# Causal masks added on VectorE within the maximum, and the two smallest query tiles scored over both branches at once

## The chip, the cores and the metric

The kernel runs on one core of a Trainium2 chip. A core has five engines that work beside each other, each through its own queue of instructions in order: TensorE (PE; its weight loads are shown apart as PEld), VectorE (DVE), ScalarE (ACT), GpSimd (POOL) and SyncE (SP), which issues DMA transfers. TensorE writes its products into PSUM, a small memory of eight banks of 2 KB per partition; everything else lives in SBUF. The metric is the time of one execution on the device in microseconds, as the median of several runs.

## The reference

One layer of a hybrid decoder is computed for two groups of tokens: a prompt of 1024 tokens, and 8 sampled sequences of 8 tokens each that have 2048 earlier tokens in a paged cache. The layer is half a SwiGLU, then a mixer of attention heads and Mamba-2 heads side by side, then another half SwiGLU. The attention has three branches that share queries: compressed blocks, selected blocks and a sliding window. What the change touches is the masked softmax of the last two, for the prompt:

```python
def masked_softmax(s, mask):
    s = jnp.where(mask, s.astype(jnp.float32), NEG)
    e = jnp.where(mask, jnp.exp(s - jnp.max(s, axis=-1, keepdims=True)), 0.0)
    return e / jnp.maximum(jnp.sum(e, axis=-1, keepdims=True), 1e-30)
...
    s = s - slopes[None, :, :, None, None] * dist      # window branch
    mask = (dist >= 0) & (dist < WINDOW) & (k_pos >= 0)[None, :]
```

There are 8 query heads over 2 key/value heads, 64 wide. The prompt has 1024 tokens in selection blocks of 64, that is 16 blocks, and 16 are selected, so that for the prompt the selected branch is plain causal attention over all earlier keys; the window branch sees the last 512. For the sampled sequences the compressed branch also needs summaries of the cached rows: blocks of 32 rows at a stride of 16 go through a small two-layer network (`compress`).

## The kernel before

**The stage.** The change lies in the attention stage, about 1130 to 1550 us of the execution. Two bodies of work are interleaved in it. The first is the prompt's attention, in 8 query tiles of 128 tokens (the program's `qt`), taken in the order 2, 7, 6, 5, 4, 3, 1, 0 (`KN["qt"]`). The second is the compression of the cached rows of the 8 sampled sequences (`compress_sample`): `KN["cs"]` = 3, 0, 2, 1, 1, 0, 1, 0 says how many sequences are written into the program ahead of each tile.

**A query tile.** First the scores of the compressed branch for all heads, `s_cmp`, with their mask (L1770) and softmax. Then for each of the 2 key/value heads and each of the two other branches (`br` 0 all earlier keys, `br` 1 the window) come the 4 query heads. A head's keys are 128(qt+1) for branch 0 and at most 640 for branch 1, cut into one or two pieces of at most 512 columns, each piece in a PSUM bank `s2` of which there are three. A piece is written by a product of the leading parts (L1808, `KA`, `QA`), a product of the small parts with the ALiBi slopes (L1810, `KB`, `QB`), and, where it has a masked block, a product of an identity with a mask in bf16 (L1813): `mdiag` for the last 128 columns, where the keys meet the queries, `medge` for the first 128 of the window. Then VectorE takes the maximum (L1818 for one piece; L1821 per piece and L1822 to join two), ScalarE the exponential straight from PSUM into the tile `pb` (L1824) with the row sums, one engine chosen by a table scales `pb` by gate and sum (L275 to L279), TensorE transposes it (L1846, `pT`), and products with the values (L1855, `o`) close the head group.

**A sequence's compression.** A gather of 128 rows of the paged cache (L1689, `chk`, one buffer), then eight times: two copies (`chp`, L267), four transposes (`cT`, L1712), the transposes' high part `th` on ScalarE (L267) and low part `tl` on VectorE (L1717), and 12 products `cA` (L1733 to L1735). After four of these the hidden layer (`cxh`) and two products `c` (L1740 for keys, L1743 for values) follow.

**What sets the order.** The program is written for a framework that lists instructions in its own order, by priorities and estimates, before the run; each engine then works through its list in order. The waits between engines follow from the tiles.

**The next stage** is the sampled sequences' attention with the output projection (`wout`, L250 to L252). Its buffers lie in the space of the compression weights `w1h` and `w1l` and of the other tiles of this stage: the window keys `schk` (L2052), the constants `big` (L1951), the residual `xT` (L1892, added to `wout` at L1939) and the weights `raw` (L1900) are loaded there.

## Time and profile before

| what | value |
|---|---|
| median of 3 runs | 2470.73 us (2468.52 to 2479.9) |
| profiled execution | 2475.45 us, its span 2473.8 us |
| mean granted clock of TensorE | 0.987 |
| busy share | PE 97%, DVE 71%, ACT 46%, POOL 17% |
| attention stage, 1130 to 1490 us | PE busy 349.4 of 360 us, DVE 226.4, ACT 235.0, POOL 143.3 |
| mask products in the stage (L1813) | 160, mean 235 and 232 ns from start to modelled end |
| maxima in the stage (L1818, L1821) | 64 and 128 |

Two readings need care. The granted clock is the share of TensorE's full speed that the chip let it have: at 0.50 every product takes twice as long, and a busy TensorE then is not one at its best. And matmuls overlap each other, so that the mean of one, as the groups show it, is longer than the time by which it delays the next; that time is read from start to start in the rows of the timeline.

### The profile page before, as it was taken

To read this page: it belongs to the slowest core of one execution; us is meant where nothing else is said; L and a number is where in the kernel's file an instruction comes from. 1 tells how busy PE (TensorE), PEld (TensorE's weight loads), DVE (VectorE), ACT (ScalarE), POOL (GpSimd) and SP (SyncE) were. 2 spreads that over 40 slices of the span, in tenths; PEclk is the share of its full clock that TensorE was granted. 3 is DMA by queue.
4 is the path that set the end of the run, shared out by engine and by line. 5 is a ranking of instruction groups with operands and counts; after the bars stand their busy time and mean duration, and the time that the engine had idled before them with its cause. 6 is when DMAs were issued, how large, how long until landed. Compare 5 with 4: busy or idle time off the path is not lost.

```text
span 2473.8 us, 48193 instructions
## 1 busy us (share of the span) xinstructions
PE 2408.8 (97%) x19026; PEld 2222.8 (90%) x19026; DVE 1744.7 (71%) x3673; ACT 1131.2 (46%) x2501; POOL 418.3 (17%) x533
## 2 busy tenths in 40 slices
PE   7999999999999999999999999999999999999998
PEld 6999999999999998997667766677899999999998
DVE  6777776677778855655656666777967676768776
ACT  7544444441133254425666675444545454543113
POOL 0000000011134343333434343111000000001110
PEclk9999999999999999999999998999999999999999
DMA  4334343598652333423110104476235353559654
GB/s 162 134 133 160 130 164 129 175 338 306 230 190 84 126 116 102 119 69 127 40 64 35 69 35 148 130 250 213 89 123 171 120 174 120 174 213 370 238 209 153
DMA packets 230446, 379.07 MB, mean 153 GB/s; under 512 B 18509, under 2 KB 147705, under 8 KB 228812
## 3 DMA queue, kind: packets, MB, share of 16 engines
q1 hardware_dynamic: 210248, 318.02, 37.7%
q0 software_dynamic: 7600, 38.59, 4.5%
q10 hardware_dynamic: 12372, 19.38, 2.2%
q8 instruction: 150, 2.46, 0.4%
q14 instruction: 76, 0.62, 0.1%
HBM read 255.66 MB, written 124.40 MB: 154 GB/s over the span
## 4 chain that ended last, share of the span: by engine, by line
PE 86%; DVE 6%; DMA 4%; ACT 3%; issue 1%; POOL 0%; ACTq 0%; DVEq 0%; POOLq 0%
PE dq L634 6%; PE gY L367 6%; PE dq L633 6%; PE dq L635 6%; PE gY L368 6%; PE gY L366 6%; PE gX L367 5%; PE gX L366 5%; PE gX L368 5%; PE o L1855 3%; PE pT L1846 3%; PE s L1808 1%; PE xbc L250 1%; PE xbc L251 1%; PE xbc L252 1%; PE cA L1733 1%
## 5 line engine op out<-in xcount | busy, mean ns | idle before, releaser
L634 PE MATMUL dq<-db,da 128*128 128x256 f32 (+1 forms) x1232 | 353.2, 288 | 0.3 <-DVE da L270 0.3
L635 PE MATMUL dq<-db,da 128*128 128x256 f32 (+1 forms) x1232 | 352.8, 288 | 0.0
L633 PE MATMUL dq<-db,da 128*128 128x256 f32 (+1 forms) x1232 | 349.8, 288 | 2.7 <-DVE Cc L386 2.2
L642 DVE TENSOR_TENSOR xT<-xT,dq 128x256 f32<-128x256 f32 (+1 forms) x456 | 186.9, 432 | 84.8 <-PE dq L635 83.2
L270 POOL TENSOR_TENSOR ds<-dw 128x512 f32<-128x512 f32 x22 | 29.5, 1341 | 1228.1 <-DVE wlo L270 508.0
L633 PEld LDWEIGHTS dq<-db,da 128*128 128x128 f32 x1232 | 230.5, 189 | 3.3 <-DVE Cc L386 2.5
L635 PEld LDWEIGHTS dq<-db,da 128*128 128x128 f32 x1232 | 232.8, 189 | 0.0
L634 PEld LDWEIGHTS dq<-db,da 128*128 128x128 f32 x1232 | 231.9, 188 | 0.6 <-DVE da L270 0.5
L267 ACT CAST whi<-ws 128x512 fp32r<-128x512 f32 x156 | 96.5, 623 | 205.9 <-PE gY L368 137.6
L270 DVE TENSOR_TENSOR wlo<-raw,whi 128x512 fp32r<-128x512 f32 x184 | 125.5, 687 | 83.9 <-ACT whi L267 83.5
L267 ACT CAST da<-ds 128x512 fp32r<-128x512 f32 x88 | 52.6, 623 | 234.7 <-PE dq L635 93.4
L267 ACT CAST whi<-raw 128x512 fp32r<-128x512 f32 x181 | 112.4, 626 | 72.0 <-PE g L414 19.5
L270 DVE TENSOR_TENSOR wlo<-ws,whi 128x512 fp32r<-128x512 f32 x156 | 106.7, 687 | 42.4 <-ACT whi L267 41.9
L1824 ACT ACTIVATE pb<-s,mx 128x256 f32<-128x256 f32 (+3 forms) x192 | 105.0, 552 | 59.7 <-DVE mx L1822 37.6
L1846 PEld LDWEIGHTS pT<-ident,pb 128*128 128x128 f32 x528 | 59.6, 143 | 45.8 <-issue 40.1
L1821 DVE TENSOR_REDUCE mx<-s 128x1 f32<-128x384 f32 (+2 forms) x128 | 66.6, 536 | 44.0 <-PE s L1813 34.1
L366 PE MATMUL gY<-B3h,whi 128*128 128x256 f32 (+1 forms) x320 | 91.5, 287 | 1.5 <-ACT whi L267 1.4
L366 PE MATMUL gX<-B6h,whi 128*128 128x256 f32 (+1 forms) x320 | 91.3, 286 | 0.9 <-ACT Cc L373 0.9
L367 PE MATMUL gX<-B6h,wlo 128*128 128x256 f32 (+1 forms) x320 | 91.4, 286 | 0.6 <-DVE wlo L270 0.6
L367 PE MATMUL gY<-B3h,wlo 128*128 128x256 f32 (+1 forms) x320 | 91.6, 287 | 0.2 <-DVE wlo L270 0.2
L277 POOL TENSOR_TENSOR pb<-pb,sm 128x640 f32<-128x640 f32 (+7 forms) x70 | 85.1, 1238 | 37.6 <-DVE sm L1831 34.0
L367 PE MATMUL gY<-B2h,wlo 128*128 128x256 f32 (+1 forms) x320 | 91.4, 286 | 0.0
(763 smaller groups left out, 8548.1 us busy)
## 6 DMA issues: line engine op xcount, KB each, us to landing
db<-GD SPq DMA_DIRECT2D x42, 1632.0 KB
GD<-Cc SPq DMA_DIRECT2D x154, 272.0 KB
GD<-his SPq DMA_DIRECT2D x84, 272.0 KB
raw<-in_ffn_wu_dram SPq DMA_DIRECT2D x22, 1024.0 KB
dw<-in_ffn_wd_dram SPq DMA_DIRECT2D x44, 512.0 KB
raw<-in_ffn_wg_dram SPq DMA_DIRECT2D x21, 1024.0 KB
GD<-hp SPq DMA_DIRECT2D x70, 272.0 KB
db<-GD SPq DMA_DIRECT2D x14, 1088.0 KB
```

Of the source, the lines that this page charges most:

```text
L267: return nc.scalar.copy(out, src) if eng == "a" else ENGINES[eng].tensor_copy(out, src)
L270: ENGINES[eng].tensor_tensor(out, x, y, op=op)
L277: nc.gpsimd.tensor_tensor(out, x, by.to_broadcast(list(x.shape)), op=OP.mult)
L366: nc.tensor.matmul(q, ah[:, k], b_, start=first, stop=False, skip_group_check=True)
L367: nc.tensor.matmul(q, al[:, k], b_, start=False, stop=False, skip_group_check=True)
L368: nc.tensor.matmul(q, ah[:, k], c_, start=False, stop=(k == 3), skip_group_check=True)
L633: nc.tensor.matmul(q, x, bh[:, u, o], start=first, stop=False, skip_group_check=True)
L634: nc.tensor.matmul(q, y, bh[:, u, o], start=False, stop=False, skip_group_check=True)
L635: nc.tensor.matmul(q, x, bl[:, u, o], start=False, stop=(u == np_ - 1), skip_group_check=True)
L642: nc.vector.tensor_tensor(x, x, q, op=OP.subtract if i == 4 else OP.add)
L1824: nc.scalar.activation(pb[:, st:st + pn], s, AF.Exp, bias=mx[:, 0:1], accum_out=part[:, hh_, i:i + 1])
L1846: nc.tensor.transpose(tq_[:kn, P * hh_:P * hh_ + P], src, ident)
```

## The change

In query tiles of three and more units of 128 keys the mask product is gone. `mrow` is one tile of 640 columns that holds `medge`, zeros and `mdiag`; a masked piece is read by a VectorE operation that adds the fitting 384 to 512 (or fewer) columns of `mrow` to the scores, negates the sum, writes it into `pb`, and returns its minimum, which is the negated maximum. The exponential reads that piece from `pb` with a scale of -1, in place. A piece without a mask is treated as before, with its maximum negated, and two pieces are joined by a minimum.

In the two smallest tiles (qt 1 and 0) both branches see the same keys in number. Their scores now go into one bank: one product takes the keys of both branches, one wider mask product serves all of the bank, and one VectorE reduction gives the maxima of 2 or 4 heads and branches; the exponentials are still one for each head and branch.

```diff
@@ -1579,10 +1579,10 @@
     Gs.close()
     Ds = ExitStack()
     AC = Ds.enter_context(pool("attc"))
-    mdiag = AC.tile([P, P], BF16, name="mdiag")
-    medge = AC.tile([P, P], BF16, name="medge")
+    mrow = AC.tile([P, 5 * P], BF16, name="mrow")
+    medge, mdiag = mrow[:, :P], mrow[:, 4 * P:]
     mcmp = AC.tile([P, 8, 64], BF16, name="mcmp")
-    for t_ in (mdiag, medge, mcmp):
+    for t_ in (mrow, mcmp):
         nc.gpsimd.memset(t_, 0.0)
     nc.gpsimd.affine_select(out=mdiag, in_=mdiag, pattern=[[-1, P]], compare_op=OP.is_ge, fill=NEG,
                             base=0, channel_multiplier=1)
@@ -1784,45 +1784,66 @@
 
             for g in range(2):
                 PT = {}
+                joint = [([], K.tile([P, 4, 2], F32, name="part", bufs=4)) for _ in range(2 if qt < 2 else 0)]
+                if joint:
+                    nk = P * (qt + 1)
+                    for h0 in range(0, 4, 2 - qt):
+                        sb = PS2.tile([P, 512], F32, name="s2", tag="s2")
+                        s = sb.rearrange("p (h b k) -> p h b k", b=2, k=nk)
+                        for u in range(2 - qt):
+                            nc.tensor.matmul(s[:, u], QAs[g][:, h0 + u], KA[:, :, g, :nk], start=(u == 0),
+                                             stop=False, skip_group_check=True)
+                            nc.tensor.matmul(s[:, u], QBq[g][:97, h0 + u], KB[:97, :, g, :nk], start=False,
+                                             stop=False, skip_group_check=True)
+                        s = sb.rearrange("p (u k) -> p u k", k=nk)
+                        n = 4 - 2 * qt
+                        nc.tensor.matmul(s[:, :, nk - P:], identb, mdiag[:, None, :].to_broadcast([P, n, P]),
+                                         start=False, stop=True, skip_group_check=True)
+                        mx = K.tile([P, NH], F32, name="mxc")
+                        nc.vector.tensor_reduce(mx[:, :n], s, axis=AX.X, op=OP.max, negate=True)
+                        for i in range(n):
+                            pbs, part = joint[i % 2]
+                            pbs.append(K.tile([P, 640 if i % 2 else 1024], F32, name=f"pb{i % 2}", bufs=5))
+                            nc.scalar.activation(pbs[-1][:, :nk], s[:, i], AF.Exp, bias=mx[:, i:i + 1],
+                                                 accum_out=part[:, h0 + i // 2, 0:1])
                 for br in range(2):
                     k0 = 0 if br == 0 else max(0, qt - 4)
                     nk = P * (qt + 1 - k0)
-                    pbs = []
+                    pbs, part = joint[br] if joint else ([], K.tile([P, 4, 2], F32, name="part", bufs=4))
                     hs_ = slice(4 * g, 4 * g + 4)
                     ns = (nk + 511) // 512
-                    part = K.tile([P, 4, 2], F32, name="part", bufs=4)
-                    for hh_ in range(4):
+                    for hh_ in range(0 if joint else 4):
                         pb = K.tile([P, 1024 if br == 0 else 640], F32, name=f"pb{br}", bufs=5)
                         pbs.append(pb)
                         st, parts = 0, []
                         for i in range(ns):
                             pn = P * ((nk // P - st // P) // (ns - i))
                             s = PS2.tile([P, 512], F32, name="s2", tag="s2")[:, :pn]
-                            parts.append((s, st, pn))
                             kk = slice(P * k0 + st, P * k0 + st + pn)
-                            masks = []
+                            mask = None
                             if st + pn == nk:
-                                masks.append((pn - P, mdiag))
-                            if br == 1 and qt >= 4 and st == 0:
-                                masks.append((0, medge))
+                                mask = mrow[:, 5 * P - pn:]
+                            elif br == 1 and qt >= 4 and st == 0:
+                                mask = mrow[:, :pn]
                             nc.tensor.matmul(s, QAs[g][:, hh_], KA[:, br, g, kk], start=True, stop=False,
                                              skip_group_check=True)
-                            nc.tensor.matmul(s, QBq[g][:97, hh_], KB[:97, br, g, kk], start=False, stop=not masks,
+                            nc.tensor.matmul(s, QBq[g][:97, hh_], KB[:97, br, g, kk], start=False, stop=True,
                                              skip_group_check=True)
-                            for j, (c, mk) in enumerate(masks):
-                                nc.tensor.matmul(s[:, c:c + P], identb, mk, start=False,
-                                                 stop=(j == len(masks) - 1), skip_group_check=True)
+                            parts.append((s, mask, pb[:, st:st + pn]))
                             st += pn
                         mx = K.tile([P, 3], F32, name="mx", bufs=4)
-                        if ns == 1:
-                            nc.vector.tensor_reduce(mx[:, 0:1], parts[0][0], axis=AX.X, op=OP.max, negate=True)
-                        else:
-                            for i in range(2):
-                                nc.vector.tensor_reduce(mx[:, 1 + i:2 + i], parts[i][0], axis=AX.X, op=OP.max)
-                            nc.vector.tensor_reduce(mx[:, 0:1], mx[:, 1:3], axis=AX.X, op=OP.max, negate=True)
-                        for i, (s, st, pn) in enumerate(parts):
-                            nc.scalar.activation(pb[:, st:st + pn], s, AF.Exp, bias=mx[:, 0:1],
-                                                 accum_out=part[:, hh_, i:i + 1])
+                        for i, (s, mask, p_) in enumerate(parts):
+                            m_ = mx[:, 1 + i:2 + i] if ns == 2 else mx[:, 0:1]
+                            if mask is None:
+                                nc.vector.tensor_reduce(m_, s, axis=AX.X, op=OP.max, negate=True)
+                            else:
+                                nc.vector.tensor_tensor_reduce(out=p_, in0=s, in1=mask, scale=-1.0, scalar=3e38,
+                                                               op0=OP.add, op1=OP.min, accum_out=m_)
+                        if ns == 2:
+                            nc.vector.tensor_reduce(mx[:, 0:1], mx[:, 1:3], axis=AX.X, op=OP.min)
+                        for i, (s, mask, p_) in enumerate(parts):
+                            nc.scalar.activation(p_, s if mask is None else p_, AF.Exp, bias=mx[:, 0:1],
+                                                 scale=1.0 if mask is None else -1.0, accum_out=part[:, hh_, i:i + 1])
                     total = part[:, :, 0]
                     if ns == 2:
                         total = sm[:, 1 + br, hs_]
```

The list of instructions changes with it. On TensorE (PE) the first scores of the first tile, `qt` 2, stood thus before:

```order
L1770 MATMUL s_cmp<-mcmp,identb 128x512
L1808 MATMUL s_14377<-KA,QA 128x384
L1810 MATMUL s_14377<-KB,QB_13182 128x384
L1813 LDWEIGHTS identb
L1813 MATMUL s_14377<-mdiag,identb 128x128
L1808 MATMUL s_14385<-KA,QA 128x384
L1810 MATMUL s_14385<-KB,QB_13182 128x384
L1813 LDWEIGHTS identb
L1813 MATMUL s_14385<-mdiag,identb 128x128
```

and now:

```order
L1770 MATMUL s_cmp<-mcmp,identb 128x512
L1828 MATMUL s_14375<-KA,QA 128x384
L1830 MATMUL s_14375<-KB,QB_13180 128x384
L1828 MATMUL s_14382<-KA,QA 128x384
L1830 MATMUL s_14382<-KB,QB_13180 128x384
L1828 MATMUL s_14389<-KA,QA 128x384
L1830 MATMUL s_14389<-KB,QB_13180 128x384
```

The mask and its weight load are gone from between the pairs. On VectorE the same heads now read:

```order
L1840 ISA pb_14374,mx<-s_14375,mrow 128x384
L1840 ISA mx 128x1
L1840 ISA pb_14381,mx<-s_14382,mrow 128x384
L1840 ISA mx 128x1
L1776 TENSOR_TENSOR pc<-s_cmp,mxc 128x512
```

Each masked piece is one operation that writes `pb`, and a short one that reads its result `mx`. In all, TensorE's list goes from 16908 to 16592 rows and VectorE's from 3337 to 3433.

At the end of the stage, TensorE's list before went from the last output products straight into the next stage (`kT_ps`, `s_ps`, `a_ps` are its sample attention):

```order
L1855 MATMUL o<-pt,VA 64x512 x2
L1855 MATMUL o<-pt,VAc 64x512
L1985 MATMUL a_ps<-gates,big 128x24
L2064 MATMUL kT_ps<-ident,schk 128x128 x8
L2096 LDWEIGHTS zrow
L2096 MATMUL so<-oneh,zrow 128x384
L1994 MATMUL a_ps<-kcTs,QS 64x127 x2
```

and now the compression of the last sequences stands behind the last output products:

```order
L1876 MATMUL o<-pt,VA 64x512 x2
L1876 MATMUL o<-pt,VAc 64x512
L1712 MATMUL cT<-ident,chp 128x128 x4
L1733 MATMUL cA<-th_13755,w1h 128x256
L1734 MATMUL cA<-th_13755,w1l 128x256
L1712 MATMUL cT<-ident,chp 128x128 x4
L1735 MATMUL cA<-tl_13756,w1h 128x256
```

with the next stage only after the last of them:

```order
L1735 MATMUL cA<-tl_13756,w1h 128x256
L1743 MATMUL c_17967<-w_179,cxh 127x64 x2
L2117 LDWEIGHTS zrow
L2117 MATMUL so<-oneh,zrow 128x384
L2085 MATMUL kT_ps<-ident,schk 128x128 x8
L2092 MATMUL s_ps<-skT,QS 64x512 x2
L250 MATMUL wout<-oh,whi 128x512 x2
```

Between these two places stand 132 products `cA` and 44 transposes `cT` in all. In the list before, the last `cA` stands ahead of the end of tiles 1 and 0.

On SP the loads of the next stage (with the semaphores that each waits for) were listed before as

```order
L2052 DMA schk<-in_cache_win_dram 128x1024 [waits DMAHW5_49,DVE_49,PE_49]
L2052 DMA schk<-in_cache_win_dram 128x1024 [waits DMAHW6_49]
L1951 DMA big<-saD 128x4552 [waits DMASW4_49,DMASW3_49,DMASW5_49,DMASW2_49,DMASW6_49,DMASW1_49,DMASW7_49,DMASW0_49,DMAHW7_49,Activation_49,Pool_49]
L1892 DMA xT_20124<-xD 128x4x256 [waits DMAHW0_49,DVE_49,PE_49]
L1892 DMA xT_20124<-xD 128x4x256 [waits DMAHW1_49]
```

and now as

```order
L2073 DMA schk<-in_cache_win_dram 128x1024 [waits DMAHW5_49,DVE_49,PE_49]
L2073 DMA schk<-in_cache_win_dram 128x1024 [waits DMAHW6_49]
L1921 DMA raw<-in_w_out_dram 128x4x128 [waits DVE_49,DMAHW7_49,PE_49,Pool_49]
L1921 DMA raw<-in_w_out_dram 128x4x128 [waits DMAHW0_49,Pool_49]
L1972 DMA big<-saD 128x4552 [waits DMASW4_49,DMASW5_49,DMASW3_49,DMASW6_49,DMASW2_49,DMASW7_49,DMASW1_49,DMAHW1_49,DMASW0_49,Pool_49]
L1913 DMA xT_19882<-xD 128x4x256 [waits DMAHW2_49]
```

The wait of the first `schk` for TensorE is in both lists one for the last `cA` (L1735); two loads of `raw` have come ahead of `big`.

## The prediction

> **What bounds the kernel now.** I read first the page's busy times and its chain of waits, then the stretches of the attention stage, then the groups of its instructions by form, and last TensorE's rows one by one around the masks and at the stage's end.
>
> ```profile
> span 2473.8 us, 48193 instructions
> PE 2408.8 (97%) x19026; PEld 2222.8 (90%) x19026; DVE 1744.7 (71%) x3673; ACT 1131.2 (46%) x2501; POOL 418.3 (17%) x533
> PE 86%; DVE 6%; DMA 4%; ACT 3%; issue 1%; POOL 0%; ACTq 0%; DVEq 0%; POOLq 0%
> ```
>
> TensorE is busy for 97% of the span and is 86% of the chain that ended last. The change touches only the attention stage, which lies at about 1130 to 1550 us. Its stretches (us, then busy time and count of PE, PEld, DVE, ACT, POOL, then the granted clock, DMA share and GB/s):
>
> ```profile
> 1130.00:1490.00 360.00, 349.37 (x2368) 255.58 (x2367) 226.36 (x519) 234.96 (x613) 143.34 (x215) 1.00 0.16 57
> 1515.00:1535.00 20.00, 18.49 (x125) 12.86 (x125) 16.58 (x54) 13.51 (x48) 7.78 (x10) 0.96 0.97 371
> 1535.00:1545.00 10.00, 10.00 (x37) 5.84 (x37) 5.89 (x25) 4.09 (x15) 4.87 (x7) 0.50 0.42 135
> 1545.00:1560.00 15.00, 13.64 (x51) 7.28 (x48) 8.62 (x27) 7.74 (x17) 0.00 (x0) 0.70 0.53 168
> ```
>
> In the body TensorE is idle for 10.6 of 360 us while VectorE (226) and ScalarE (235) have a third of the time free. So work taken from TensorE there shortens the stage, as long as the other two keep up. The stage's end is another matter: from 1515 to 1560 TensorE loses 1.5 + 1.4 us idle, and by the granted clock (20 x 0.04) + (10 x 0.50) + (15 x 0.30) = 10.3 us: some 13 us in all. The DMA share of 0.97 there is the next stage's loads, which start when the last compression product frees their space and so run under tiles 1 and 0.
>
> **Part 1, the mask products (saves TensorE time).** Groups by form within the attention stage (busy, mean ns of one, idle before):
>
> ```profile
> L1813 PE MATMUL s<-mdiag,identb 128*128 128x128 bf16 x128 | 30.1, 235 | 0.0
> L1813 PE MATMUL s<-medge,identb 128*128 128x128 bf16 x32 | 7.4, 232 | 0.0
> L1821 DVE TENSOR_REDUCE mx<-s 128x1 f32<-128x512 f32 x24 | 16.2, 686 | 11.1 <-PE s L1813 8.0 <-PE s L1810 3.0
> L1818 DVE TENSOR_REDUCE mx<-s 128x1 f32<-128x128 f32 x16 | 4.4, 285 | 3.1 <-PE s L1813 2.9
> L1818 DVE TENSOR_REDUCE mx<-s 128x1 f32<-128x256 f32 x16 | 6.2, 413 | 0.9 <-PE s L1813 0.9
> ```
>
> There are 160 mask products. 128 of them stand in tiles of three and more units and go; the 32 of the two smallest tiles become 12 wider ones. The mean of 235 ns is latency, since matmuls overlap; what one costs is read from start to start:
>
> ```profile
> 1300.92 0.23 PE L1813 MATMUL s<-medge,identb 128*128 128x128 bf16 x1
> 1300.96 0.36 PE L1733 MATMUL cA<-th,w1h 128*128 128x256 f32 x1
> 1301.16 0.28 PE L1734 MATMUL cA<-th,w1l 128*128 128x256 f32 x1
> 1301.28 0.49 PE L1712 MATMUL cT<-ident,chp 128*128 128x128 f32 x3
> ...
> 1515.18 0.23 PE L1813 MATMUL s<-mdiag,identb 128*128 128x128 bf16 x1
> 1515.24 0.83 PE L1846 MATMUL pT<-ident,pb 128*128 128x128 f32 x6
> ```
>
> The next product starts 0.04 us after the mask, but then takes 0.20 us to its successor where the same form takes 0.12: a mask between float products costs 0.04 + 0.08 = 0.12 us. Ahead of transposes it costs 0.06. I take 0.095, between these, as both successors are frequent: (160 - 12) x 0.095 = **14 us** (bounds 148 x 0.04 = 6 to 148 x 0.12 = 18).
>
> **Part 2, the two smallest tiles.** Their 32 pairs of score products become 8 pairs of 512 columns (tile 1) and 8 of 256 (tile 0). The columns stay the same in number, and about half the per-product overhead goes; their masks are wider. I work it out at **-1.2 us** on TensorE (bounds -3 to +1), by 0.14 + 0.12 for a pair of 128, 0.20 + 0.12 for 256 and 0.32 + 0.24 for 512, estimates from the same start-to-start reading. On VectorE 16 x 0.285 + 16 x 0.413 = 11.2 us become 12 x 0.686 = 8.2.
>
> **Part 3, VectorE and ScalarE.** The new operation adds the mask, takes the extreme and writes the piece back in one pass. The trace has no such operation; the nearest rows are a custom one that also reads two operands, writes a tile and returns a sum:
>
> ```profile
> L2080 DVE CUSTOM_DVE_ANT_0 S<-s_ps,big x20: 660/688/692, 1555.8 to 1721.1; 128x512 f32<-128x512 f32 x20
> L2080 DVE DVE_READ_ACCUMULATOR2_ANT smxs<- x20: 75/83/88, 1556.4 to 1721.7; 128x1 f32 x20
> ```
>
> 688 against 686 ns for the plain reduction of 512 says that the pass itself costs nothing more, and that each gets an 83 ns reading of the accumulator: 128 x 0.083 = +10.6 us, with the joint tiles' -3.0 together +7.7 us, against 360 - 226 = 134 us free. It is hidden on the whole; where three heads are scored in a burst it isn't, since the exponential waits for the maximum. Bounds 0 and +7.7 on the path (if every one of them were waited for); I take **+1**, nearest to the mean share that is free. ScalarE now reads these pieces from SBUF; with 125 us free I cost that at nothing, and it would add some 4 us of ScalarE time if the cover were gone. On the other side the score bank is now free after VectorE's pass and not after the exponential:
>
> ```profile
> PE s L1808 <- ACT pb L1824: 3.8, 10, 0.7
> ```
>
> This wait of TensorE, with the same one on its weight loads, is 12 us at most in the stage. Bounds 0 to 8 us; I take **-3**, since the remaining unmasked pieces still wait for the exponential.
>
> **Part 4, the end of the stage (moved work).** By the order of the changed kernel the compression of the last sequence no longer lies before tiles 1 and 0: after the last output product there still stand 132 products cA with 44 transposes cT and the last products c. Nothing is added, about 20 us of TensorE work only moves behind the tiles. But there it is alone, and its own chain sets the pace:
>
> ```profile
> L1712 PE MATMUL cT<-ident,chp 128*128 128x128 f32 x256 | 41.3, 276 | 2.0 <-DVE mx L1822 1.0 <-DVE tl L1717 0.7 <-ACT chp L267 0.3
> L267 ACT CAST th<-cT 128x512 fp32r<-128x512 f32 x64 | 37.5, 586 | 26.2 <-PE cT L1712 25.8
> L1717 DVE TENSOR_TENSOR tl<-cT,th 128x512 fp32r<-128x512 f32 x64 | 44.0, 687 | 16.6 <-ACT th L267 16.1
> ...
> 1452.77 0.39 POOL L267 COPY chp<-chk 128x256 f32<-128x256 f32 x1
> ...
> 1463.22 0.40 POOL L267 COPY chp<-chk 128x256 f32<-128x256 f32 x1 [0.90 <-DMA chk<-in_cache_cmp_dram,idx]
> ```
>
> A pair's cycle is cT (some 0.6) + th 0.59 + tl 0.69 = 1.9 to 2.0 us, against 12 x 0.118 + 0.45 = 1.9 us of TensorE work, so the pairs themselves hardly stall. Between two sequences the gather shows: 1463.22 - 1452.77 = 10.45 us from the last copy of one to the first of the next, in which about 5 us of products are left over: 5 us idle. The hidden layer (activations and a multiplication before c), twice, and the start of the chain cost about 1.6 + 1.65 + 2.4 = 5.6 us more. And an idle stretch of this sort has its price in clock, as the 0.50 of 1535 to 1545 shows; I add 3 us. Together **13.6** (bounds 6 and 17).
>
> The Trainium skill, "TensorE: Matmul & The Clock Gate", section "What's actually happening", says that the clock gate halves the rate after an idle window of about 3.4 us and opens after a busy one. By that page, an estimate, each idle stretch that fills a window would cost 1.7 us or more. This trace has 0.50 already after stalls of only about 1 us, so it is harder than the page.
>
> What is late next are the loads of the following stage, since their buffers lie in the compression weights' space:
>
> ```profile
> SPq L2052 <- PE cA L1735: 382.6, 1, 382.6
> ...
> 1514.90 0.83 SPq L2052 DMA_DIRECT2D schk<-in_cache_win_dram  x2
> 1518.58 10.61 SPq L1892 DMA_DIRECT2D xT<-xD  x4
> ```
>
> The SP queue waits for the last cA and starts at 1514.9; after it the DMA share stays near 1 until 1535, that is 20 us at 371 GB/s. Now these 20 us start behind the last cA, with no tile to cover them. In order the first window keys are there 5 us later, the 2276 KB of big after 12 to 19, xT after 22 to 25. TensorE can do until then the window transposes and scores and only the first 24 output projections, since the residual they are added to is xT:
>
> ```profile
> 1562.81 0.39 PE L252 MATMUL wout<-ol,whi 128*128 128x512 f32 x1
> 1563.04 0.39 PE L250 MATMUL wout<-oh,whi 128*128 128x512 f32 x1
> ...
> L2022 DVE TENSOR_TENSOR cm<-imp x4: 1153/1161/1161, 1562.4 to 1685.0; 128x961 f32<-128x961 f32 x4
> ```
>
> 24 x 0.23 = 5.6 us, with the transposes about 10 us. Behind the loads VectorE still has a chain of 1.16 us operations, so TensorE's next long run starts at 28 to 30 us: **18.5 us** idle, and 2 for the clock (bounds 5, if the loads go faster and everything fits beneath them, and 20).
>
> New end 13.6 + 18.5 + 2 = 34 us, old end 13: **+20.5** (bounds 0 and +26).
>
> **The sum.** -14 - 1.2 - 3 + 1 + 20.5 = +3.3 us. It is made against the profiled execution of 2475.45 us, 4.7 above the median of 2470.73; on the median it gives 2474 us. About 0.5%, 12 us, is what a measurement of this kernel can tell from no change.
>
> **The rivals.** *A, the end eats the gain (the sum):* 2474 us, no change that can be told. For it speaks that the loads really lasted 20 us and wait for the last cA; against it that the exact position of each start is estimated.
>
> *B, the end costs little:* the loads are spread, or the boundaries fit under the left-over work, and the end costs only its lower bound and a little more, +3. Then 2470.7 - 18 + 1 + 3 = 2457 us. For it: SP has free queues and DMA is at 0.16 in the body. Against it: the wait of 382.6 us is on the space, not on a queue.
>
> *C, slower:* the loss at the end is at its upper bound (+26), and the masks save only 10 (more stand before transposes than I assume), with no gain at the score banks: 2470.7 - 10 - 1 + 3 + 26 = 2489 us. The mechanism is the single one of exposed loads behind a serial compression; it decides for slower as soon as the end costs over 31 us with the full saving of 18, or over 23 with a saving of 10.
>
> *D, VectorE becomes the bound in the score bursts:* the full +7.7 and 83 ns more in each chain from score to exponential, 128 x 0.083 = 10.6 at most. With A that is 2474 + 9 = 2483 us; against it speak the 134 us that are free. *E, the change doesn't do what it says* (the scheduler gives TensorE something else to wait for in place of the masks): as the sum without its first term, 2488, within C's reach.
>
> **How the numbers follow.** A 0.47, B 0.25, C with E 0.18, D 0.10. The likeliest is A, 2474 us, whose own range is 2463 to 2482. With B's 2457 and C's 2489 at the ends the range is **2456 to 2491**. Faster by over 0.5% means below 2458.4: most of B and a little of A, 0.24. Slower means above 2483.1: C, E and half of D, and A's upper tail, 0.29. Same 0.47.
>
> **What would show it.** The mask products at 12 where they were 160, with the body from 1130 to 1490 some 14 us shorter: parts 1 and 2. The plain reduction replaced by one of equal duration with an accumulator reading of about 83 ns: part 3. The last cA after the last o product, TensorE idle for several us at the sequence boundary, SP's first key load directly behind the last cA and the DMA share near 1 for 20 us with TensorE mostly idle, at half clock: part 4. If the loads start while tiles 1 and 0 still run, or TensorE is busy through them, part 4 is wrong and B holds; if the new operation takes clearly more than 0.69 us at 512, part 3 is.

## The result, and the profile after

The changed kernel takes 2501.29 us (median of four runs, 2500.15 to 2503.92), the kernel before 2471.18 us. The ratio is 1.0117, with a 95% interval of 1.0096 to 1.0138: 30 us slower. The prediction had 2474 us, in a range that ended at 2491.

The head of the page of the changed kernel, with a span 25.4 us longer than before (the execution profiled before stood 4.3 us above its median):

```profile
span 2499.2 us, 47952 instructions
## 1 busy us (share of the span) xinstructions
PE 2403.2 (96%) x18846; PEld 2221.9 (89%) x18846; DVE 1748.1 (70%) x3781; ACT 1134.5 (45%) x2501; POOL 419.4 (17%) x532
```

TensorE is busy for 5.6 us less in a longer span; the time was lost in waits and, within the busy time, at half clock. Four stretches of the changed kernel (us, busy time of PE, PEld, DVE, ACT and POOL, granted clock, DMA share, GB/s): the body, the tail from the last output product to the last product `c`, from there to the 96th product of the output projection, and the rest of the next stage.

```profile
1130.00:1490.00 360.00, 347.76 (x2249) 253.45 (x2247) 249.28 (x693) 249.36 (x662) 144.64 (x214) 0.99 0.14 51
1505.80:1546.00 40.20, 28.46 (x188) 24.69 (x186) 14.04 (x28) 14.81 (x33) 8.32 (x14) 0.87 0.21 71
1546.00:1607.80 61.80, 47.69 (x279) 33.15 (x279) 28.77 (x73) 17.47 (x38) 6.93 (x8) 0.78 0.63 223
1607.80:1777.30 169.50, 158.93 (x1524) 121.84 (x1523) 129.41 (x357) 80.07 (x178) 23.90 (x22) 0.95 0.65 207
```

The same two later stretches of the kernel before, from the start of its last tile's scores to the 96th product of the projection and on to the 576th:

```profile
1521.90:1588.00 66.10, 63.82 (x352) 42.74 (x351) 46.11 (x136) 30.71 (x83) 6.88 (x10) 0.85 0.53 180
1588.00:1753.30 165.30, 157.34 (x1574) 121.03 (x1573) 131.18 (x366) 81.51 (x183) 24.68 (x24) 0.98 0.67 214
```

Idle time and lost clock together, the clock summed over its records: 12.5 us in the end of the stage before, 44.6 us (16.9 in the tail, 27.7 behind it) now. In the rest of the next stage they grew from 11.4 to 19.1 us, and from the stage's start to these stretches from 12.9 to 18.1 us. The tail's 16.9 us are 11.7 us idle and 5.1 us of lost clock (rounded), the 27.7 us behind it 14.1 us idle and 13.7 us of lost clock.

The tail itself, TensorE's rows of the changed kernel that waited (at the right the idle time before them and what ended it):

```profile
1506.94 0.39 PE L1733 MATMUL cA<-th,w1h 128*128 128x256 f32 x1 [0.86 <-ACT th L267]
1509.04 0.63 PE L1712 MATMUL cT<-ident,chp 128*128 128x128 f32 x4 [1.59 <-DVE tl L1717]
...
1517.82 0.62 PE L1743 MATMUL c<-w,cxh 128*127 128x64 f32 x4 [1.56 <-DVE cxh L1414]
1521.32 1.12 PE L1712 MATMUL cT<-ident,chp 128*128 128x128 f32 x4 [2.88 <-ACT chp L267]
...
1545.43 0.63 PE L1743 MATMUL c<-w,cxh 128*127 128x64 f32 x4 [1.56 <-DVE cxh L1414]
1547.60 2.30 PE L2085 MATMUL kT_ps<-ident,schk 128*128 128x128 f32 x8 [1.28 <-DMA schk<-in_cache_win_dram]
...
1555.48 0.79 PE L250 MATMUL wout<-oh,whi 128*128 128x512 f32 x1 [2.94 <-ACT whi L267]
1560.10 0.80 PE L250 MATMUL wout<-oh,whi 128*128 128x512 f32 x1 [3.82 <-ACT whi L267]
...
1571.29 0.76 PE L2027 MATMUL a_ps<-spc,big 128*128 128x127 f32 x2 [2.67 <-DVE spc L2024]
```

The waits that part 4 of the prediction named are there: the low parts, the hidden layer, the gather between two sequences, and the window keys. One is there that it did not name: the first products of the projection, which it let run beneath the loads, waited 2.94 and 3.82 us for their own weights. `whi` comes from `raw`, of which two loads were issued just ahead of `big`; they landed while `big` and `xT` were loading too. TensorE shows no wait for `xT`, which part 4 took for the limit. SP's list starts 0.3 us behind the last `cA`, where it started under tile 1 before:

```profile
1543.90 0.83 SPq L2073 DMA_DIRECT2D schk<-in_cache_win_dram  x2
1546.12 0.94 SPq L1921 DMA_DIRECT2D raw<-in_w_out_dram  x2
1547.42 0.34 SPq L1972 DMA_DIRECT2D big<-saD  x1
1547.81 16.36 SPq L1913 DMA_DIRECT2D xT<-xD  x4
```

And the new operation, in the groups by form:

```profile
L1840 DVE CUSTOM_DVE_ANT_0 pb<-s,mrow 128x384 f32<-128x384 f32 x64 | 34.6, 550 | 6.6 <-PE pT L1867 4.7 <-PE s L1830 1.7
L1840 DVE CUSTOM_DVE_ANT_0 pb<-s,mrow 128x512 f32<-128x512 f32 x32 | 21.5, 686 | 6.1 <-PE s L1830 4.0 <-PE pT L1867 1.8
L1840 DVE DVE_READ_ACCUMULATOR2_ANT mx<- 128x1 f32 x128 | 10.5, 82 | 0.0
L1845 ACT ACTIVATE pb<-pb,mx 128x384 f32<-128x384 f32 x64 | 38.7, 606 | 10.3 <-DVE mx L1840 10.3
```

It takes 550 ns at 384 columns and 686 at 512, as the plain reduction did (553 and 686), and 82 ns more for its result. The exponential from SBUF takes 606 ns where it took 577 from PSUM.

### The profile page after: what moved, and what is told of

It is laid out like the page before. It is cut to its first block, busy times and chain, and to the rows that moved or that the text cites. A ratio compares the mean times of both kernels' runs of the same rounds, so it can differ in the third digit from the quotient of the medians.

```text
span 2499.2 us, 47952 instructions
## 1 busy us (share of the span) xinstructions
PE 2403.2 (96%) x18846; PEld 2221.9 (89%) x18846; DVE 1748.1 (70%) x3781; ACT 1134.5 (45%) x2501; POOL 419.4 (17%) x532
## 4 chain that ended last, share of the span: by engine, by line
PE 85%; DVE 7%; DMA 4%; ACT 2%; issue 2%; POOL 0%; SPq 0%; ACTq 0%; DVEq 0%; POOLq 0%
PE gY L367 6%; PE gY L366 6%; PE gY L368 6%; PE dq L633 6%; PE dq L634 6%; PE dq L635 6%; PE gX L367 5%; PE gX L366 5%; PE gX L368 5%; PE o L1876 3%; PE pT L1867 3%; PE xbc L250 1%; DMA db<-GD 1%; PE xbc L251 1%; PE xbc L252 1%
## 5 line engine op out<-in xcount | busy, mean ns | idle before, releaser
L366 PE MATMUL gY<-B2h,whi 128*128 128x256 f32 (+1 forms) x320 | 91.4, 286 | 0.0
L368 PE MATMUL gY<-B3l,whi 128*128 128x256 f32 (+1 forms) x320 | 91.3, 286 | 0.0
```

What stands on the lines that cost most here:

```text
L366: nc.tensor.matmul(q, ah[:, k], b_, start=first, stop=False, skip_group_check=True)
L368: nc.tensor.matmul(q, ah[:, k], c_, start=False, stop=(k == 3), skip_group_check=True)
```

## The experiments

Two questions stood open: is the loss the order, in which the compression slid behind the tiles, or the VectorE operation; and why does the saved TensorE work not show? All ratios below are to the kernel before, in the same session, with 95% intervals. Beside them stands the length of the stage in the profiled execution, from the first compressed score to the last of the next stage's 576 products of the projection: 616.8 us before, 641.0 us changed. What lies ahead of it is the same list of instructions in all kernels, and took between 1133 and 1144 us in the 19 profiles, so that spans of single profiles tell little under 6 us.

**One part alone.** The joint tiles without the rest, and the changed kernel without any masks in the larger tiles:

```diff
 # joint_only: tiles of three and more units as before
-                            if st + pn == nk:
-                                mask = mrow[:, 5 * P - pn:]
-                            elif br == 1 and qt >= 4 and st == 0:
-                                mask = mrow[:, :pn]
+                            if st + pn == nk:
+                                masks.append((pn - P, mdiag))
+                            if br == 1 and qt >= 4 and st == 0:
+                                masks.append((0, medge))
...
+                            for j, (c, mk) in enumerate(masks):
+                                nc.tensor.matmul(s[:, c:c + P], identb, mk, start=False, ...)
 # no_masks: mask is None for every piece
```

> Only the two smallest tiles changed (joint scores); the larger tiles keep their mask products on TensorE. In its order the compression ends ahead of the last tiles, as in the kernel before. Tail theory (the loss of the changed kernel comes from the compression that slid behind the tiles): no tail, so only the -1.2 us of the small tiles, 2470 us, within 3 us of the kernel before. Rival, the joint tiles themselves lose time (fewer, longer exponential chains on three score banks): 5 us or more slower, 2476 us or above.

> The changed kernel with the masks of tiles of three and more units left out altogether: neither the mask product nor the VectorE operation, but a plain maximum, and the exponential from PSUM; the scores of masked keys are thus not masked. In its order the compression ends ahead of the last tiles. It prices the 128 mask products by themselves. Tail theory: 14 + 1.2 us less than before, 2456 us, with the same end of the stage as before. Rival, a mask product costs only its own issue of 0.04 us: 128 x 0.04 + 1 = 6 us less, 2465 us. Rival, something else than TensorE bounds this stage: no gain, 2471 us.

Measured: joint_only 1.0018 (1.0005 to 1.0031), stage 615.5 us; no_masks 1.0060 (1.0043 to 1.0077), stage 620.8 us. None of the three theories of no_masks held. Its profile shows that the work did shrink, by busy time less lost clock in the stage from 580.0 to 568.0 us, 12 us where the prediction's terms for it gave 15. (This measure is rough: kernels with the same products as the one before differ by 5.5 us in it, those with the changed kernel's by 11.) But idle time grew from 21.5 to 28.9 us and lost clock from 15.4 to 23.9: 16 us came back for 12 saved, in a kernel with no VectorE masks and no tail at all. So leaving products out didn't shorten this stage by itself. Its list differs from the one before by more than the masks, though: up to 26 products of the compression stand further ahead. And the profiled stage holds 4 us of the 14 us by which its median is longer. joint_only is 1.3 us shorter in its profiled stage, too little for one profile to tell, and its median is 4.5 us above; where those lie its profile does not show.

**The order moved by other engines.** Three copies of the compression on other engines, so that the list has it earlier:

```diff
-'chp': 'ap', 'th': 'aa'
+'chp': 'va', 'th': 'av'
```

> The changed kernel with three copies of the compression given to other engines (one half of the gathered rows' copies from ScalarE to VectorE, the other from GpSimd to ScalarE, every second th from ScalarE to VectorE). By its order 12 products cA are left ahead of the last output products and none behind them, where the changed kernel has 132 behind. Tail theory: the serial tail of 39 us goes, but the loads of the next stage still start only at the end of the tiles, so some 10 to 20 of the 24 us at the end come back: 2478 us, between 2466 and 2488. Rival, the VectorE operation itself is what costs (its accumulator reads and its place in the chain from score to exponential): the loss stays and grows by VectorE's new copies, 2500 us or above.

> The kernel before with the same three copies moved as in the run after_early; its order still ends the compression ahead of tile 0, some 10 products earlier. It is the control of that run: the moved copies lie on engines with a third of the time free, so no change is expected, 2471 us, within 5 us. If it comes out faster or slower by more, that difference is to be taken off the reading of after_early.

Measured: after_early 1.0059 (1.0039 to 1.0079), stage 619.4 us; before_early 1.0047 (1.0030 to 1.0063), stage 625.7 us. The tail is gone from after_early and with it 18 us of the 30, so at least these aren't the operation's. The control lost 12.6 us by the same copies and an order that ends much like the old one; with that taken off, as its expectation asks, nothing of the loss is left in after_early, which is 12.2 us above the kernel before.

**The tail alone, and the order forced.** before_tail puts the eighth sequence's compression behind the last output product of the kernel before. The three others force the compression ahead by edges within TensorE's own list, which are no waits on the chip:

```diff
 # before_tail
-'cs': [3, 0, 2, 1, 1, 0, 1, 0]
+'cs': [3, 0, 2, 1, 1, 0, 0, 0]
+                        if b == 7 and kv == jj == u == g == 0:
+                            tc.add_manual_dep(tr.ins, last_o[0].ins.name, ...)   # first cT behind the last o
...
+        compress_sample(7)
 # after_forced, before_forced: need = [0, 0, 2, 4, 5, 7, 8, 8]
 # after_forced_late:           need = [0, 0, 2, 4, 5, 6, 7, 8]
+                if h == 0 and need[qi]:
+                    tc.add_manual_dep(sc.ins, lastca[need[qi] - 1].ins.name, ...)
```

> The kernel before, with its masks on TensorE, but the eighth sequence's compression listed behind the last output product: 96 products cA and 32 transposes alone at the end, and the loads behind them, without any VectorE mask. Order theory: the end loses what it lost in the changed kernel (27.7 us from the last cA on, some 9 us in the tail of one sequence) against 12.5 us before: 2471 + 24 = 2495 us, between 2485 and 2505. Rival, the loss of the changed kernel belongs to the VectorE operation: no more than 5 us over the kernel before, 2476 us.

> The changed kernel, with the engines of all operations as they are, but with its order forced: the first compressed score of a query tile is listed behind the last cA of the 2nd, 4th, 5th, 7th and 8th sequence (third to seventh tile). In its order the compression now ends ahead of tile 1, as before the change. Order theory (the loss is the compression and the loads that slid behind the tiles): the end of the stage is that of the kernel before, and the removed products remain: 2471 - 14 to 18 + 4 for the longer waits in the body, 2458 us, between 2450 and 2466. Rival, the VectorE operation costs as much as it saves wherever it stands: 2471 us or above. Rival, any move of the order away from the kernel before costs 5 to 12 us, as the runs no_masks and before_early showed: 2465 to 2472 us.

> As after_forced, but the seventh sequence is asked for ahead of the seventh tile and the eighth only ahead of the last one: the compression ends between tiles 1 and 0, and the next stage's loads have only tile 0, some 25 us, to lie beneath. Order theory: 2 to 8 us slower than after_forced, since the loads last about 20 us and start with tile 0; 2463 us. Rival, the loads' cover does not matter: the same as after_forced within 2 us.

> The kernel before with the same forced order, the control of after_forced: its compression ends one tile earlier than it did. Order theory: the loads start some 15 us earlier beneath the tiles, 0 to 5 us less than before, 2469 us. Rival, any move of the order costs: 2476 to 2484 us.

Measured: before_tail 1.0175 (1.0157 to 1.0194), stage 649.2 us. Its end, from the last output product to the 96th product of the projection, and the rest:

```profile
1537.50:1625.00 87.50, 66.36 (x414) 49.42 (x412) 40.29 (x96) 28.72 (x63) 12.35 (x17) 0.82 0.48 166
1625.00:1793.50 168.50, 157.62 (x1524) 121.32 (x1523) 131.03 (x360) 80.09 (x178) 23.14 (x22) 0.96 0.66 208
```

That is 21 us idle and a clock of 0.82 in the end, and the same growth of the rest of the next stage, 168.5 us against 165.3, as in the changed kernel (169.5). No mask is on VectorE here. So the tail alone costs more than the whole loss of the change (43 us, where 24 were expected).

after_forced came out at 1.0065 (1.0048 to 1.0082), stage 632.4 us; after_forced_late at 1.0002 (0.9991 to 1.0014), stage 614.7 us; before_forced at 1.0049 (1.0032 to 1.0065), stage 625.8 us. Forcing the compression ahead of the last tile takes the whole 30 us back. Forcing it one tile earlier costs 16 us again, against the expectation. The loads then have more cover, but in tiles 4, 3 and 1 idle time and lost clock of TensorE came to 15.7 us, where after_forced_late has 0.7; tile 0 and the end did not lose more (14.1 us against 15.2). after_forced has all the compression ahead of tile 1 and none within it. The control lost 13 us by its forced order too.

**The clock.** The prediction had 5 us of lost clock for the new end, and the profile shows 18.8 there. after_filled puts idle products into the stalls, so that the clock stays up; late_filled does it in after_forced_late.

```diff
+    def warm(q, n, after=None):
+        for _ in range(n):
+            mm = nc.tensor.matmul(q[:, :512], identb, identb[:, None, :].to_broadcast([P, 4, P]), start=True, stop=True, ...)
+            if after is not None:
+                tc.add_manual_dep(mm.ins, after.ins.name, ...)
...
                 q = b1("c2")
+                warm(q, {(6, 1): 6, (7, 0): 6, (7, 1): 6}.get((b, kv), 0), lastca[b])
...
+            warm(q, (11, 15)[...], ...)          # first two groups of wout
```

> The changed kernel in its own order, with products of no use (an identity with itself, 128x512 in bf16, into banks that the next product overwrites) put into the stalls of TensorE from the compression's tail to the first output projections: 6 before each of the last three c, 11 before the last sequence's first cT, 5 and 2 before the first kT_ps and s_ps, 11 and 15 before the first two groups of wout, 10 before the sample's second a_ps. They compute nothing that is read. Clock theory (the idle time itself is as predicted, and the half clock that follows each stall is what the prediction undersized): the granted clock stays near 1 from 1505 to 1608 us, where 18.8 us were lost, and 12 to 15 us come back: 2488 us. Rival, the stalls set the time whatever the clock is: 2501 us, within 3 us. Rival, such products do not hold the clock or lengthen the stalls: above 2503 us.

> after_forced_late (the changed kernel with the compression's end forced between tiles 1 and 0) with the same sort of products at two stalls: 8 before the first transposes of tile 0 (2.0 us of stall, followed by 13.7 us at half clock) and 4 before the first kT_ps (1.0 us of stall, 6.8 us at half clock). Clock theory: up to 10 us of lost clock come back, less some 1 us by which the fillers overshoot: 2465 us, under both kernels. Rival, the stall is the price and not the clock: 2473 us, within 3 us.

Measured: after_filled 1.0068 (1.0042 to 1.0094), stage 635.6 us; late_filled 1.0030 (1.0016 to 1.0045), stage 624.8 us. The end of the changed kernel and of after_filled, from the last output product to the 96th product of the projection:

```profile
1505.80:1607.80 102.00, 76.16 (x465) 57.84 (x464) 42.81 (x101) 32.28 (x71) 15.25 (x21) 0.82 0.46 163
```

```profile
1511.50:1613.40 101.90, 87.93 (x542) 60.59 (x541) 45.11 (x103) 33.24 (x71) 14.46 (x21) 0.95 0.47 163
1613.40:1777.40 164.00, 156.20 (x1519) 121.55 (x1518) 128.94 (x356) 78.16 (x176) 23.31 (x22) 0.96 0.66 214
```

The clock rose from 0.82 to 0.95, the idle time fell from 25.8 to 14.0 us, and in this profile the end took 102 us all the same. That speaks for the rival, by which gathers, loads and the copies between engines set its time. It does not settle it. The fills cost time themselves: the 15 ahead of the projection's second group ran from 1566.3 to 1569.4 us, although that group's weights were ready at 1565.1. And the profiled execution, 2498.56 us, is the slowest of four; the ratio fell from 1.0117 to 1.0068, some 12 us, which is what the clock theory expected. In the profile the stage is 5.4 us shorter, and these lie behind the end, 164.0 us against 169.5, where there are no fills. How much of the end the slow clock set stays open. late_filled was meant to beat both kernels and is 7 us over after_forced_late. Its end is 61.4 us, from the start of the last tile to the 96th product, against 64.1, but its list of the next stage came out in another order, and the rest took 179.5 us against 166.6:

```profile
1524.40:1585.80 61.40, 54.22 (x308) 35.36 (x306) 41.38 (x111) 27.45 (x76) 10.37 (x13) 0.94 0.63 227
1585.80:1765.30 179.50, 166.87 (x1588) 126.46 (x1587) 135.47 (x377) 83.47 (x189) 25.23 (x24) 0.93 0.63 199
```

```profile
1521.40:1585.50 64.10, 59.14 (x308) 38.09 (x307) 43.08 (x119) 29.68 (x81) 10.40 (x13) 0.84 0.62 221
1585.50:1752.10 166.60, 159.15 (x1575) 123.67 (x1574) 132.17 (x369) 82.00 (x183) 24.23 (x24) 0.96 0.67 213
```

**What the masks are worth when the order is forced.** Two kernels with the edges of after_forced_late, one without masks and one with the masks on TensorE, and two that imitate the old order (by their profiles to 26 products `cA`):

```diff
 # before_forced_late and no_masks_late: need = [0, 0, 2, 4, 5, 6, 7, 8]
 # after_old_order, masks_old_order (the latter without joint tiles)
+                if h == 0:
+                    behind_pair(sc, [0, 1, 16, 29, 41, 53, 59, 64][qi])
...
+                                if ui == len(units) - 1 and u == 0:
+                                    behind_pair(mm, [(1, 5), (11, 17), (25, 32), (38, 45), (49, 56), (56, 56), (64, 64), (64, 64)][qi][g])
```

> As after_forced_late, but the masks of tiles of three and more units are left out altogether (plain maxima, exponentials from PSUM; the scores of masked keys are not masked). The difference from after_forced_late is what the VectorE operation itself costs. Theory: nothing but the 10.6 us of accumulator readings on an engine with time free, 2473 us within 4 us. Rival, the operation's place between score and exponential costs the 8 to 10 us by which after_forced_late misses the saving of the products: 2463 us.

> The kernel before with the order forced as in after_forced_late (the eighth sequence ahead of the last tile). The difference from after_forced_late is what the masks on VectorE are worth when the order is held. Theory: 10 to 16 us of TensorE products, less what comes back as stalls in the body: 2479 us, 4 to 8 us above after_forced_late. Rival, nothing is saved once stalls and clock are counted: 2473 us.

> The changed kernel, all operations on their engines, with the compression's place forced to that of the kernel before: at each tile's compressed scores and at each head group's last output products, as many pairs of the compression must be listed ahead as were listed there (to 12 products). The loads of the next stage follow in the old order too. If the order accounts for the whole loss: the masks' and the small tiles' gain at equal order, as before_forced_late and after_forced_late gave it (9 to 11 us), 2471 - 10 = 2461 us, below both kernels. Rival, the shorter tiles need another order, and any with these masks stalls by what it saved, as after_forced_late did: 2472 us, within 3 us. Rival, the VectorE operation has a cost of its own that the order hid: 2476 us or above.

> As after_old_order, but without the joint scores of the two smallest tiles: these have a product, a mask on VectorE, and a maximum for each head and branch. The difference is what the joint tiles are worth. Prediction's term: joint scores save 1.2 us of TensorE, and their masks are here on VectorE too, which saves 12 more of them: 1 to 2 us around after_old_order. Rival, the joint tiles lose some 4 us, as joint_only came out against the kernel before: 4 us faster than after_old_order.

Measured: no_masks_late 1.0043 (1.0029 to 1.0057), before_forced_late 1.0044 (1.0030 to 1.0057), after_old_order 1.0056 (1.0037 to 1.0075), masks_old_order 1.0023 (1.0011 to 1.0036).

With the late edges the kernel with masks on VectorE is 0.42% faster (1.0002 against 1.0044), 10 us, than the one with masks on TensorE, and also 10 us faster than the one without masks. The second difference can't be the masks' worth, since that kernel has less to do, and the first isn't shown to be either: the edges say what must stand ahead of a tile, and not what must stand behind it. Products `cA` ahead of the last four tiles' first scores, counted in the profiles:

| kernel | tile 4 | tile 3 | tile 1 | tile 0 |
|---|---|---|---|---|
| before | 480 | 636 | 708 | 768 |
| after_forced_late, masks_forced_late, part_ge4 | 480 | 576 | 672 | 768 |
| before_forced_late | 504 | 672 | 732 | 768 |
| no_masks_late | 504 | 660 | 732 | 768 |
| part_ge6 | 516 | 660 | 720 | 768 |

So before_forced_late and no_masks_late, both slower than their expectations had it, were not run in the order of after_forced_late. Against the kernel before, after_forced_late has 561.7 us of work where that had 580.0, and 53.0 us idle or lost to the clock where that had 36.8; 10.7 of these 16 us came back ahead of the last tile.

Near the old order the masks on VectorE lose: the stage is 621.4 us in after_old_order, and not 10 us less than 616.8. The work is 570.6 us there against 580.0, and the waits took it back. masks_old_order, without the joint tiles, is 0.33% faster than after_old_order, 8 us, twice what the rival expected, but its profiled stage is as long (621.7 us). TensorE's waits from the second tile to the last one, first in the kernel before, then in after_old_order (us in total, times, longest):

```profile
PE s L1808 <- ACT pb L1824: 2.3, 6, 0.7
PE cA L1733 <- ACT th L267: 1.7, 3, 0.7
PE c L1743 <- DVE cxh L1414: 1.1, 2, 0.6
PE pT L1846 <- ACT pt L267: 1.0, 2, 0.6
PE cT L1712 <- DVE mx L1822: 1.0, 1, 1.0
PE cT L1712 <- DVE tl L1717: 0.7, 1, 0.7
PE pT L1846 <- DVE pt L267: 0.4, 1, 0.4
```

```profile
PE s L1839 <- DVE mx L1851: 4.5, 5, 2.2
PE pT L1878 <- ACT pt L267: 3.5, 4, 1.4
PE cT L1719 <- DVE tl L1724: 2.8, 4, 1.8
PE pT L1878 <- DVE pt L267: 2.4, 5, 0.9
PE cA L1742 <- DVE tl L1724: 1.7, 1, 1.7
```

Scores wait for the new operation to free their bank (4.5 us, where the wait for the exponential was 2.3), and transposes and compression wait for their copies on VectorE and ScalarE: 14.9 us in these five rows against 8.2 us in all seven before.

**A part of the masks, and the joint tiles.** At the late forced order, all masks on VectorE without joint tiles; and masks on VectorE only in the larger tiles:

```diff
 # masks_forced_late: no joint tiles
-                joint = [... for _ in range(2 if qt < 2 else 0)]
+                joint = [... for _ in range(0)]
 # part_ge4, part_ge6: on VectorE only if qt >= 4, or qt >= 6; on TensorE otherwise
+                                if qt >= 4:
+                                    mask = mrow[:, 5 * P - pn:]
+                                else:
+                                    masks.append((pn - P, mdiag))
```

> after_forced_late without the joint tiles (all masks on VectorE, each head and branch of the small tiles by itself). If the joint tiles lose some 5 us, as masks_old_order against after_old_order has it: 2468 us. If they are worth the 1.2 us of the prediction or nothing: 2473 to 2475 us.

> As masks_forced_late, but masks are on VectorE only in the tiles of five and more units (96 of the 128 pieces); the smaller tiles keep theirs on TensorE. VectorE theory (the saved products come back as waits for VectorE, above all at the stage's start, where the first tile has little beside it): the first tile's waits shrink by some 3 us, and 3 us of products come back: the same as masks_forced_late within 2 us, 2468 to 2473 us. Rival, what is lost is lost by the order alone: the same order, the same time less nothing, plus 3 us, 2476 us.

> Masks on VectorE only in the two largest tiles (48 of the 128 pieces), the order forced as before: the compression then ends ahead of tile 0 as in before_forced_late. VectorE theory: less added to VectorE's list, less saved, 2475 us, between before_forced_late and masks_forced_late. Rival, the order alone decides: as before_forced_late, 2482 us.

Measured: masks_forced_late 1.0001 (0.9990 to 1.0011), stage 612.0 us; part_ge4 1.0035 (1.0023 to 1.0047), stage 620.2 us; part_ge6 1.0065 (1.0040 to 1.0089), stage 626.4 us. The joint tiles change nothing that can be told at this order (1.0001 against 1.0002). Both part kernels came out slower than either of their theories had it. part_ge6 has another order, as the table shows, and can't be compared. part_ge4 and masks_forced_late have the compression in the same places to 12 products, and differ by 64 masks; with all masks on VectorE the time is 0.34% shorter, 8 us, so the theory that VectorE's load takes the saved products back falls for this pair. But of the 8.2 us of the profiled stage 2.8 lie up to the 96th product of the projection, and 5.4 behind it, where none of these masks stand and the list differs. What the masks alone are worth is not shown.

No kernel beat the one before: masks_forced_late and after_forced_late equal it.

## Why the prediction was wrong

**The sum, by its own steps.** In the profiled stage the change is +24.2 us (616.8 to 641.0); the rest of the spans' 25.4 lies outside the stage. By busy time less lost clock, TensorE's work fell by 20.8 us (580.0 to 559.2), where parts 1 and 2 had 15.2 (a rough measure, as said above). The end lost 44.6 us where 12.5 were lost before: +32.1, and part 4 had +20.5. The body lost 18.1 against 12.9, +5.1, where part 3 had -2 (-3 for the score banks and +1). The rest of the next stage lost 19.1 against 11.4, +7.7, and the prediction had no term there. -20.8 + 32.1 + 5.1 + 7.7 = +24.1.

**What was right.** The operation's time and its accumulator reading (82 ns, forecast 83), the exponential from SBUF, and the mechanism of part 4, seen in the order alone: the serial tail, the wait of SP for the last `cA`, and the bare loads. The old end was put at 13 us and was 12.5. before_tail shows that this order costs the time without any mask on VectorE, and after_forced_late that without it the loss is gone. Rival C named the direction and its condition, over 31 us at the end with the full saving (32.1 were measured). It got 0.18 with E, and its 2489 us are 12 us short of the 2501.29 measured.

**What failed, step by step.**

The first, and the largest, is the size of the end in part 4, 34 us forecast and 44.6 measured, and within it the term for the clock: 3 + 2 us were put down, 18.8 were lost (5.1 in the tail, 13.7 behind it), while the idle time was overrated, 10.6 + 18.5 us against 11.7 + 14.1. The tail was put at 13.6 us lost and was 16.9. A pair of the compression alone took 2.12 us from one `th` to the next at full clock, not 1.9 to 2.0, as two rows of ScalarE's timeline of the changed kernel show:

```profile
1529.83 0.59 ACT L267 CAST th<-cT 128x512 fp32r<-128x512 f32 x1 [1.24 <-PE cT L1712]
...
1531.95 0.59 ACT L267 CAST th<-cT 128x512 fp32r<-128x512 f32 x1 [1.23 <-PE cT L1712]
```

The stretch behind it was put at 18.5 + 2 and was 27.7, where its upper bound was 20. Its path was wrong in part: the 24 products that were to run beneath the loads waited for their weights, 2.94 and 3.82 us at the first two groups, then TensorE waited for the sample's softmax, 2.67 us, and for the residual `xT` it shows no wait. The 20.5 us were a sum of single waits along a chain, with the slow clock set small. Whether the lost clock made the end longer or only filled waits is open: after_filled took 11.8 us of idle time and most of the lost clock out of it, its profiled end stayed at 102 us, and its median fell.

The second is the lack of a term for what comes after. The stretch from the 96th to the last product of the projection lost 7.7 us more. before_tail, where it lost 17.7 us against 11.4, shows much of the same growth without any VectorE mask. That the sample's attention starts late there, against a projection that else fills its waits, is our reading and was not tested.

The third is the premise of the first part: "work taken from TensorE there shortens the stage, as long as the other two keep up". TensorE was busy in 97% of the body, and still no_masks, which has 12 us less work and no new operation, was not faster but 14 us slower, and none of the kernels with 48 to 180 fewer products in their lists came out faster than the one before. We read it so that the busy share was high because the list in use had filled the waits of two chains, scores to exponentials to transposes, and the compression's, with each other's work, and that with the products taken out the waits are bare again. No run shows this by itself, since no run took the products out of a list that else stayed as it was. The order alone costs as much: before_early, before_forced and before_forced_late lost 11 to 13 us with the same products on TensorE as the kernel before.

The fourth is the -3 us for the score banks in part 3. TensorE's waits and its weight loads' waits for a bank, 3.8 + 8.5 us for the exponential before, became 4.7 + 8.6 us for the new operation (who waited for the exponential before, then for the new operation; us, times):

```profile
  PEld s L1808: 8.5, 15
  PE s L1808: 3.8, 10
...
  PEld s L1828: 8.6, 15
  PE s L1828: 4.7, 7
```

Nothing was gained: the bank comes free after VectorE's pass, as was said, but TensorE waited for that pass as long as it had for the exponential.

The range failed with these: it took the end's upper bound as +26, and 39.8 us (32.1 + 7.7) was lost there and after it. A loss had a chance of 0.29, although the list already showed 132 products out from under their cover.

**What stays open.** What the masks on VectorE are worth when nothing else changes: they came out at -0.4% in one pair whose orders differ by up to 96 products (after_forced_late and before_forced_late), at -0.3% in one that agrees to 12 (masks_forced_late and part_ge4), and at +0.2% (masks_old_order) and +0.6% (after_old_order) near the old order. The joint tiles came out at 0, +0.2 and +0.3% in three orders. Some orders that differ little are 5 to 14 us apart, and no single wait in their profiles accounts for it. Whether an order exists in which the saved products show in full was not found.

## What to carry to other kernels

Before pricing an edit by the work it removes, compare the lists of instructions before and after, and look for work that has lost its cover: what stands alone at a stage's end, and which loads wait for it. Where an engine is busy for 97% because a tuned list hides two latency chains under each other, an operation less on it can be worth nothing; a run that leaves the operation out altogether is a cheap first test, if its list is compared with the old one too. Edges that force an order bound it from one side only: count where the other work stands before two such kernels are compared. A stretch that waits for loads and copies is priced from the last release to the first long run of work, the stage behind it included, not as a sum of single idle times.

## What the runs showed of the hardware

In the records of these profiles TensorE's granted clock drops by half for stretches of 3.4 us and multiples of it. In the changed kernel this happened after a stall of 2.2 us between two products (1192.2 to 1195.6 us), and for 17.1 us after the stalls of 1.56 and 1.28 us at the stage's end; in the kernel before, stalls of 0.67 and 0.25 us were followed by 13.7 us at half clock, although TensorE showed no idle time between 1535 and 1545. The Trainium skill, "TensorE: Matmul & The Clock Gate", section "What's actually happening", has the clock fall after an idle window of some 3.4 us and come back after a busy one: the windows' length agrees with these records, the idle time that was enough here is shorter, and the 10 us of busy time from 1535 to 1545 did not bring the clock back. Idle products in the stalls kept the clock at 0.95 where it was 0.82; the profiled stretch was no shorter for it.

The two forms of VectorE's work, the plain maximum and the one that adds a mask, writes the tile and returns the extreme, took the same time within 3 ns at 384 and 512 columns.
